# Modulation streams beside an output projection: earlier start, two row tiles a step, half of them on TensorE

## The chip, the cores and the metric

The kernel runs on one core of a Trainium2 chip. The metric is the device time of one execution in microseconds (us); the time of a kernel is the median of its runs. TensorE multiplies matrices, VectorE (DVE), ScalarE (ACT) and GpSimd (POOL) work element by element, SyncE (SP) issues most of the DMA transfers. Each engine takes its own instructions strictly in the order in which they stand in the program, and waits in front of one whose operands are not there yet.

## What is computed

Two layers of a diffusion backbone over 512 latent tokens and 256 context tokens, width 1024, all in 32-bit floats. Layer 0 is a mixer (retention and mLSTM heads) and then a gated feed-forward part. Only the seam between the two matters here:

```
mod = silu(c) @ ada_w[layer] + ada_b[layer]            # 1024 -> 6*1024, the same for c_ctx
sh1, sc1, g1, sh2, sc2, g2 = split(mod, 6)
x   = x + g1 * (concat(retention, mlstm) @ ab_w_out)   # the mixers' output projection
h   = rmsnorm(x, norm_w) * (1 + sc2) + sh2
x   = x + g2 * ((silu(h @ w_gate) * (h @ w_up)) @ ffn_w_out)
```

The same three lines are computed for the context tokens with c_ctx. sc2 and sh2 (columns 32 to 39 and 24 to 31 of the 48 column tiles of mod) are first needed behind the output projection, in the norm ahead of the feed-forward part.

## The kernel before

**Products.** A 32-bit product is made of three TensorE products of rounded parts: each operand is split into a high part (a cast on ACT) and a low part (the rest, a subtraction on DVE). So each 128-column weight unit is loaded by DMA into one of three buffers `wr` (512 KB), cast to `wh` on ACT and subtracted to `wl` on DVE, with three buffers of each.

**The output projection** is `op_out` (from line 1487). It goes through the latent tokens (`LAT`, 512 columns) and then the context tokens (`CTX`, 256 columns); in each, through eight output tiles k. A step is one tile: 8 row tiles by 3 products make 24 matmuls into one PSUM bank `pf`, and `evac` on DVE adds the gated bank to the residual stream `xt`; ACT then squares the new rows and POOL sums the squares into `nacc` for the norm. There are two banks, so step k + 2 waits for the evacuation of step k.

**The modulation streams** (`ada_stream`, from line 700). One stream makes eight column tiles of mod: its weight rows come as eight row tiles `aw` of 128 x 1024 (512 KB each, three buffers, issued on SP). For a row tile k in `on_pe`, TensorE does it directly (`ada_round`: four matmuls of 32 x 256, one for each quarter of the columns). For any other, DVE multiplies the tile by a scalar per partition and adds it to one of two sums `acc` (one for c, one for c_ctx): two instructions of 128 x 1024. In the end two more rounds on TensorE (`ones`) sum each `acc` over the partitions into the same bank `ada`; ACT copies the bank, DVE transposes it and adds the bias (`mod`) and for sc2 the norm weight (`amod`). Streams run one after another. Before, `op_out` starts the stream for sc2 (32) behind step 2 and that for sh2 (24) behind step 5 of LAT, each with row tiles 0 and 1 on TensorE and six on DVE.

**The norm ahead of the feed-forward part** (`norm_seven0`): POOL takes the root of the sums (`rs`), TensorE spreads it over the partitions (`nbc`), DVE writes rows times scale into four tiles `bb` and ACT adds the shift sh2 in place; then come the forms: `two` casts a form's high part on ACT and subtracts its low part on DVE into tiles `g`. The form b11 is the first quarter (upper rows, first 256 columns), b21, b12 and b22 are the others.

**The feed-forward part** begins with `plain()`: two units of gate and up columns, 192 matmuls of 256 columns into `pu`, first with b11 and b21, then with b12 and b22; behind them the context product `pc`. Their weights come through `wr` again, split into `xh`, `xl` (gate) and `wh`, `wl` (up).

**Order of the work.** The program is written by generators that a planner (`Flow`) interleaves by its own estimates of cost, and the tile framework's scheduler may move instructions again when the program is built. So the order on each engine is fixed at build time but stands in no line of the source.

Of the kernel before, what the change touches and what calls it, by code (L numbers as in the profile page):

```python
# [15 lines left out]
P = 128  # L16
# [127 lines left out]
def kernel(ctx, tc, x, c, cx, c_ctx, ada_w, ada_b, norm_w, ffn_w_in, ffn_w_out, ab_w_in,  # L144
# [15 lines left out]
    def nm(s):  # L160
        seq[0] += 1
        return f"{s}_{seq[0]}"
# [3 lines left out]
    def big(shape, dt, name):  # L166
        slots.n -= 1
        return bigp.tile(shape, dt, tag="big", name=nm(name))
# [3 lines left out]
    def psum(name="ps", tag="mx"):  # L172
        return psp.tile([P, 512], F32, tag=tag, name=nm(name))
# [7 lines left out]
    def bank(name):  # L181

        return psum(name, "pj")
# [12 lines left out]
    def order(inst, prev):  # L196
        if prev is not None:
            tc.add_manual_dep(inst.ins, prev.ins.name,
                              mybir.DependencyInfo(mybir.DependencyClass.NoSync, mybir.DependencyReason.DATA),
                              reason="groups of one bank in turn")  # L200
# [10 lines left out]
    def steps(o, pairs, prev=None, cut=12):  # L211

        n = len(pairs)
        m = None
        for i, (l, r) in enumerate(pairs):
            m = pe.matmul(o, l, r, start=(i == 0), stop=(i == n - 1))
            if i == 0:
                order(m, prev)
            if i % cut == cut - 1 and i < n - 1:
                yield  # L220
        return m
# [155 lines left out]
    for i, (lo, hi) in ((1, (2, 4)), (2, (4, 6)), (0, (0, 2))):  # L377
# [4 lines left out]
        for kk in range(4):  # L382
# [3 lines left out]
            for j in range(2):  # L386
                for b in range(2):
                    k = 2 * kk + j
# [221 lines left out]
    def op(gen, specs=()):  # L610

        W.plan(specs)
        prog.append(gen)

    def wfeat(src):
        return src, KT, P

    def pairs_feat(w, c0, ah, al, a, b, ks=KT):
        res = []
        h_, l_ = w  # L620
        for k in range(ks):
            wh, wl = h_[:, k, c0:c0 + P], l_[:, k, c0:c0 + P]
            h, lo = ah(k, a, b), al(k, a, b)
            res += [(wh, h), (wh, lo), (wl, h)]
        return res
# [20 lines left out]
    def evacuated():  # L646

        evac_t.append(flow.cur.t)
        flow.cur.t = evac_t[-2] if len(evac_t) > 1 else 0.0
# [25 lines left out]
    def op_feat(src, acts, evac, parts=(LAT, CTX), before=None, after=None):  # L675

        def gen():
            if before is not None:
                yield from before()
            u, = yield from W.take(1)  # L680
            for part in parts:
                a, b, mc = part
                ps = bank("pf")
                yield from steps(ps[:, 0:b - a], pairs_feat(u, 0, *acts(), a, b))
                if part is parts[-1]:
                    W.give(1)
                evac(part, ps[:, 0:b - a])
                evacuated()
                yield
            if after is not None:  # L690
                after()
        op(gen, [wfeat(src)])
# [3 lines left out]
    def ada_unit():  # L696

        if len(ada_ring["units"]) == 0:
            ada_ask()
        return ada_ring["units"].pop(0)  # L700

    passed, pace = [0], [0]

    def ada_stream(turn, l, t0, on_pe=range(KT), gap=0.0, cols=2, freed=0, every=0):

        yield lambda: ada_turn[1] == turn
        ps = None
        acc = [None] * 2  # L710
        for k in range(KT):
            if every:
                yield lambda: passed[0] >= pace[0]
                pace[0] = max(pace[0], passed[0]) + every
            u, at = ada_unit()
            flow.cur.t = max(flow.cur.t, at)
            yield
            if k in on_pe:
                first = ps is None
                if first:  # L720
                    ps = psum("ada")
                ada_round(ps, k, u, start=first, stop=len(on_pe) == KT and k == KT - 1)
            else:
                for i in range(cols):
                    new = acc[i] is None
                    if new:
                        acc[i] = ada_ring["acc"]()
                    s_ = cmod[:, k, i:i + 1]
                    if new:
                        z = dve.tensor_scalar(acc[i], u, s_, None, ALU.mult)  # L730
                    else:
                        z = dve.scalar_tensor_tensor(acc[i], u, s_, acc[i], ALU.mult, ALU.add)
                    order(z, flow.main)
            slots.n += freed
            ada_ask()
            flow.cur.t = flow.T["pe"] + gap
            yield
        first = ps is None
        if first:
            ps = psum("ada")  # L740
        for i in range(cols if len(on_pe) < KT else 0):
            ada_round(ps, 0, acc[i], ones[:, i, :], first and i == 0, i == cols - 1)
        ada_end(l, t0, KT, ps)
        ada_turn[1] += 1

    def op_ada(l, t0, **how):
        def gen():
            flow.add(ada_stream(ada_turn[0], l, t0, **how), 4, "ada")
            ada_turn[0] += 1
            yield  # L750
        op(gen)
        ada_ring["plan"] += [ada_w[l, P * k:P * k + P, P * t0:P * t0 + D] for k in range(KT)]
# [729 lines left out]
    def op_wait(cond):  # L1482
        def run():
            yield cond
        op_do(run)

    def op_out(wsrc, acts, l, gk, parts, then, adas=()):

        adas = list(adas)
        op_wait(lambda: {(l, 8 * gk), (l, 8 * gk + 4)} <= ada_done)  # L1490
        for part in parts:
            for k in range(KT):
                def evac(part, ps, k=k):
                    a, b, mc = part
                    dve.scalar_tensor_tensor(xk(xt, k, a, b), ps, mod[l][:, 8 * gk + k, mc:mc + 1],
                                             xk(xt, k, a, b), ALU.mult, ALU.add)
                    square_sum(k, a, b)
                op_feat(wsrc[:, P * k:P * k + P], acts, evac, (part,))
                if adas and k % 3 == 2:
                    op_ada(l, adas.pop(0), on_pe=(0, 1))  # L1500
            then(part)

    ready = {}
# [40 lines left out]
    def norm_seven0():  # L1544

        a, b, mc = LAT
        ps2 = psum("nsum")
        for i in range(a // P, b // P):
            pe.matmul(ps2[:, i:i + 1], nacc[:, P * i:P * i + P], cst[:, C_INV:C_INV + 1], start=True, stop=True)
        bcs = yield from rms_bc((ps2[:, a // P:b // P], a // P))  # L1550
        yield lambda: {(0, 24 + t) for t in (0, 4, 8, 12)} <= ada_done
        bb = []

        def two(name, q, src):
            h, lo = form0(0, name, q), form0(1, name, q)
            act.copy(h, src)
            dve.tensor_tensor(lo, src, f(h), ALU.subtract)

        for q in range(4):
            bb.append(big([P, 3, NL], F32, "bb"))  # L1560
            for k in range(2):
                kk = 2 * q + k
                dve.scalar_tensor_tensor(bb[q][:, k], xk(xt, kk, a, b), amod[0][:, 1, kk, 0:1], bcs, ALU.mult, ALU.mult)
                act.activation(bb[q][:, k], bb[q][:, k], AF.Identity, bias=mod[0][:, 24 + kk, 0:1])
        four = [(bb[q][:, 0:2, 0:256], bb[2 + q][:, 0:2, 0:256], bb[q][:, 0:2, 256:512], bb[2 + q][:, 0:2, 256:512],
                 bb[q][:, 2].rearrange("p (k n) -> p k n", k=2)) for q in range(2)]
        for q, (b11, b21, b12, b22, t2) in enumerate(four):
            two("b11", q, b11)
        done0.add("b11")
        yield lambda: "mixed" in done0  # L1570
        for name, i in (("b21", 1), ("b12", 2), ("b22", 3)):
            for q in range(2):
                two(name, q, four[q][i])
            done0.add(name)
            yield
        yield lambda: 0 in done0
        for q, (b11, b21, b12, b22, t2) in enumerate(four):
            dve.tensor_tensor(b11, b11, b12, ALU.subtract)
            dve.tensor_tensor(t2, b22, b11, ALU.add)
        for name in ("t2", "t3", "n1", "n4"):  # L1580
            for q, (b11, b21, b12, b22, t2) in enumerate(four):
                if name == "t3":
                    dve.tensor_tensor(b12, b12, b22, ALU.subtract)
                if name == "n4":
                    dve.tensor_tensor(b21, b21, t2, ALU.subtract)
                two(name, q, {"t2": t2, "t3": b12, "n1": b11, "n4": b21}[name])
            done0.add(name)
            yield
# [827 lines left out]
```

## Time and profile before

| | us |
|---|---|
| median of 3 runs | 1760.28 (1760.05 to 1765.24) |
| profiled execution, its own time | 1761.57 |
| its span, first to last instruction | 1759.8 |
| TensorE busy | 1688.9 (96%) |
| DVE busy | 1213.0 (69%) |
| ACT busy | 754.0 (43%) |
| output projection of layer 0, first to last matmul | 469.8 to 554.1 |
| of it the latent steps | 469.8 to 518.5 |
| first context product of the feed-forward part | 587.6 |

The stage in question is the 118 us from 469.8 to 587.6. A busy share tells little here, since TensorE is busy over most of the span: what counts is where it is idle or at its lower clock, and which instruction ends each such stretch. Matmul rows overlap, so the price of a matmul is the distance between two starts, not its duration.

### The profile page before, as it was taken

Reading aid. Unit: us, or ns where it says so; the run is one execution under the profiler, and the core shown is the slowest. Engines: PE = TensorE matmul, PEld = TensorE weight load, DVE = VectorE, ACT = ScalarE, POOL = GpSimd, SP = SyncE. Lnnn points to the kernel's source line nnn. Section 1 sums busy time; section 2 is a strip of 40 time slices with the busy share of each in tenths; the row PEclk is TensorE's granted clock in tenths of the full one; section 3 lists DMA queues with packets and bytes.
Section 4 is the critical chain, followed back from the end, with each engine's and each line's share of the span. In section 5 each row is a group of like instructions: output and inputs, shape, how many; then the busy total and the mean of one; then the engine's idle time right before and its main releaser. Section 6 shows DMA issues by size and latency. Waiting matters only on the chain.

```text
span 1759.8 us, 31421 instructions
## 1 busy us (share of the span) xinstructions
PE 1688.9 (96%) x12770; PEld 1551.6 (88%) x12770; DVE 1213.0 (69%) x2112; ACT 754.0 (43%) x1406; POOL 305.7 (17%) x308
## 2 busy tenths in 40 slices
PE   7899999999998999999999999799999899999998
PEld 5799899999877998999999998799778899999998
DVE  4845365756588795876657475769765788778785
ACT  4532344433424533333444333545665554344343
POOL 4212120201023001000010102426564300000000
PEclk9999999999999999999999999999999999999999
DMA  9511111011477247466564835322002523333335
GB/s 339 207 52 49 37 37 49 25 37 54 162 217 226 61 144 164 124 167 157 147 164 147 205 122 184 113 73 70 4 1 93 160 73 105 103 105 97 108 86 155
DMA packets 230324, 203.34 MB, mean 116 GB/s; under 512 B 8172, under 2 KB 207268, under 8 KB 230180
## 3 DMA queue, kind: packets, MB, share of 16 engines
q1 hardware_dynamic: 222468, 178.20, 33.1%
q0 software_dynamic: 5760, 18.88, 5.5%
q10 hardware_dynamic: 1952, 4.27, 0.7%
q8 instruction: 100, 1.64, 0.4%
q14 instruction: 44, 0.36, 0.1%
HBM read 178.25 MB, written 23.07 MB: 114 GB/s over the span
## 4 chain that ended last, share of the span: by engine, by line
PE 63%; issue 14%; DVE 10%; DMA 6%; ACT 4%; POOL 2%; SPq 0%; POOLq 0%; ACTq 0%; DVEq 0%
PE pf L107 20%; PE pu L107 12%; PE pt L107 10%; PE pg L107 4%; PE pc L107 4%; DMA wr<-in_ffn_w_in_dram 3%; PE sc L107 3%; DVE acc L107 2%; PE mo L107 2%; PE ao L107 2%; DVE wl L107 2%; DMA xs<-stage 1%; PE atr L107 1%; PE ro L107 1%; PE kv L107 1%
## 5 line engine op out<-in xcount | busy, mean ns | idle before, releaser
L107 PE MATMUL pf<-fu,wh 128*128 128x512 f32 (+1 forms) x1152 | 293.2, 345 | 8.4 <-DVE xt L107 2.8
L107 PEld LDWEIGHTS pf<-fu,wh 128*128 128x128 f32 x1152 | 198.1, 190 | 38.8 <-ACT wh L107 4.7
L107 DVE TENSOR_TENSOR wl<-wr,wh 128x1024 fp32r<-128x1024 f32 (+1 forms) x144 | 173.1, 1203 | 71.4 <-ACT wh L107 69.6
L107 ACT CAST wh<-wr 128x1024 fp32r<-128x1024 f32 (+1 forms) x144 | 143.8, 1001 | 178.7 <-PE pf L107 68.1
L107 PE MATMUL pf<-fu,wl 128*128 128x512 f32 (+1 forms) x576 | 196.0, 342 | 0.0
L107 DVE TENSOR_TENSOR wl<-ws,wh 128x1024 fp32r<-128x1024 f32 x80 | 97.4, 1221 | 57.1 <-ACT wh L107 56.5
L107 PE MATMUL pu<-g,wh 128*128 128x256 f32 x704 | 130.4, 283 | 1.9 <-DVE hfull L107 1.9
L107 ACT CAST xh<-wr 128x1024 fp32r<-128x1024 f32 x84 | 78.4, 946 | 120.6 <-DMA wr<-in_ffn_w_in_dram 71.1
L107 PE MATMUL pc<-g,xh 128*128 128x256 f32 x672 | 123.0, 282 | 1.2 <-ACT stage L107 0.8
L107 ACT CAST wh<-ws 128x1024 fp32r<-128x1024 f32 x80 | 83.5, 1050 | 94.8 <-PE pu L107 47.8
L107 PEld LDWEIGHTS pf<-fu,wl 128*128 128x128 f32 x576 | 109.0, 189 | 13.5
L107 DVE SCALAR_TENSOR_TENSOR acc<-aw,cmod,acc 128x1024 f32<-128x1024 f32 x90 | 117.9, 1335 | 0.1
L107 PE MATMUL pu<-hT,wh 128*128 128x256 f32 x640 | 115.3, 280 | 0.0
L107 PEld LDWEIGHTS pu<-g,wh 128*128 128x128 f32 x704 | 108.9, 190 | 3.4 <-DVE hfull L107 2.1
L107 DVE TENSOR_TENSOR xl<-wr,xh 128x1024 fp32r<-128x1024 f32 x84 | 91.7, 1096 | 21.5 <-ACT xh L107 21.3
L107 PEld LDWEIGHTS pc<-g,xh 128*128 128x128 f32 x672 | 104.1, 190 | 2.0 <-ACT stage L107 1.6
L107 PE MATMUL pu<-g,wl 128*128 128x256 f32 x352 | 99.9, 284 | 0.8 <-DVE wl L107 0.7
L107 PEld LDWEIGHTS pu<-hT,wh 128*128 128x128 f32 x640 | 97.7, 188 | 0.7 <-ACT hT L107 0.2
L1774 POOL DMA_DIRECT2D xs<-stage x32 | 27.9, 871 | 400.2 <-ACT stage L107 381.0
L107 PE MATMUL pc<-g,xl 128*128 128x256 f32 x336 | 94.5, 281 | 0.0
L107 PE MATMUL pu<-hT,wl 128*128 128x256 f32 x320 | 87.7, 281 | 1.5 <-DVE wl L107 1.5
L107 PE MATMUL pt<-wh,hh 128*128 128x256 f32 x288 | 83.3, 291 | 4.1 <-ACT hh L107 2.7
(388 smaller groups left out, 4833.5 us busy)
## 6 DMA issues: line engine op xcount, KB each, us to landing
wr<-in_ffn_w_in_dram SPq DMA_DIRECT2D x88, 512.0 KB, 3.9
aw<-in_ada_w_dram SPq DMA_DIRECT2D x84, 512.0 KB, 5.3
wr<-in_ab_w_in_dram SPq DMA_DIRECT2D x32, 512.0 KB, 4.5
wr<-in_ffn_w_out_dram SPq DMA_DIRECT2D x32, 512.0 KB, 4.1
xs<-stage POOLq DMA_DIRECT2D x32, 384.0 KB, 6.1
wr<-in_ffn_w_out_dram SPq DMA_DIRECT2D x32, 384.0 KB, 4.2
wr<-in_ab_w_out_dram SPq DMA_DIRECT2D x16, 512.0 KB, 4.2
wr<-in_attn_w_out_dram SPq DMA_DIRECT2D x16, 512.0 KB, 4.2
```

Of the source, the lines that this page charges most:

```text
L107: r = fn(*a, **k)
L1774: nc.gpsimd.dma_start(xs2[k // 2, :, NT * (k % 2):NT * (k % 2) + NT], stage[0][:, k % 2], accum_op=ALU.add)
```

## The change

Three things change. `op_out` counts a step in `passed` after each tile and starts the two streams ahead of steps 0 and 1 instead of behind steps 2 and 5. Each stream takes row tiles 0 to 3 on TensorE (before 0 and 1), four on DVE (before six), and with `every=0.5` its row tile k may go on only when int(k / 2) steps have passed since the stream began: two row tiles a step. In `norm_seven0` the rows of `bb` are written in the order in which the forms need them: rows 0 and the b11 forms of them, rows 1 and theirs, then rows 2 and 3; before, all four first.

```diff
@@ ada_stream
         for k in range(KT):
-            if every:
+            if 0 < every < 1:
+                p0 = passed[0] if k == 0 else p0
+                yield lambda: passed[0] >= p0 + int(every * k)
+            elif every:
                 yield lambda: passed[0] >= pace[0]
                 pace[0] = max(pace[0], passed[0]) + every
@@ op_out
+        def step():
+            passed[0] += 1
+
...
-                op_feat(wsrc[:, P * k:P * k + P], acts, evac, (part,))
-                if adas and k % 3 == 2:
-                    op_ada(l, adas.pop(0), on_pe=(0, 1))
+                if adas and k < 2:
+                    op_ada(l, adas.pop(0), on_pe=range(4), every=0.5)
+                op_feat(wsrc[:, P * k:P * k + P], acts, evac, (part,), after=step)
@@ norm_seven0
         for q in range(4):
             bb.append(big([P, 3, NL], F32, "bb"))
+
+        def rows(q):
             for k in range(2):
                 kk = 2 * q + k
...
         for q, (b11, b21, b12, b22, t2) in enumerate(four):
+            rows(q)
             two("b11", q, b11)
         done0.add("b11")
+        for q in (2, 3):
+            rows(q)
         yield lambda: "mixed" in done0
```

Up to the first matmul of the output projection the order of every engine is the same as before. **DVE, from the first evacuation of the output projection on** (`xt<-pf` is an evacuation, `wl` the low part of a weight unit, `acc` a row tile of a stream). Before:

```order
L107 SCALAR_TENSOR_TENSOR xt_4889<-pf_5157,mod_173,xt_4889 128x512
L107 TENSOR_TENSOR wl_5221<-wr_5025,wh_5219 128x1024
L107 SCALAR_TENSOR_TENSOR xt_4889<-pf_5190,mod_173,xt_4889 128x512
L107 TENSOR_TENSOR wl_5256<-wr_5087,wh_5254 128x1024
L107 TENSOR_SCALAR acc_5273<-aw_5152,cmod 128x1024
L107 TENSOR_SCALAR acc_5275<-aw_5152,cmod 128x1024
L107 SCALAR_TENSOR_TENSOR xt_4890<-pf_5225,mod_173,xt_4890 128x512
```

Now:

```order
L107 SCALAR_TENSOR_TENSOR xt_4889<-pf_5157,mod_173,xt_4889 128x512
L107 TENSOR_TENSOR wl_5218<-wr_5025,wh_5216 128x1024
L107 TENSOR_SCALAR acc_5256<-aw_5201,cmod 128x1024
L107 TENSOR_SCALAR acc_5258<-aw_5201,cmod 128x1024
L107 SCALAR_TENSOR_TENSOR acc_5256<-aw_5226,cmod,acc_5256 128x1024
L107 SCALAR_TENSOR_TENSOR acc_5258<-aw_5226,cmod,acc_5258 128x1024
L107 SCALAR_TENSOR_TENSOR xt_4889<-pf_5203,mod_173,xt_4889 128x512
```

The first stream's sums stand one step earlier, and an evacuation of a latent step now stands behind four of them. The last `acc` of the second stream stands ahead of the seventh latent evacuation; before, it stood behind the second context evacuation.

**TensorE, between the sixth and the seventh context step** (`pf_5745` and `pf_5759` are the sixth step's bank, `pf_5780` and `pf_5788` the seventh's, `pu` the feed-forward part's first product). Before:

```order
L107 MATMUL pf_5745<-ml_5139,wh_5723 128x256
L107 MATMUL pf_5745<-mh_5138,wl_5725 128x256
L107 MATMUL pf_5780<-mh_4897,wh_5758 128x256
L107 MATMUL pf_5780<-ml_4898,wh_5758 128x256
L107 MATMUL pf_5780<-mh_4897,wl_5760 128x256
```

Now:

```order
L107 MATMUL pf_5759<-ml_5139,wh_5718 128x256
L107 MATMUL pf_5759<-mh_5138,wl_5720 128x256
L107 MATMUL pu_5883<-g_905_5636,xh_5836 128x256
L107 MATMUL pf_5788<-mh_4897,wh_5753 128x256
L107 MATMUL pf_5788<-ml_4898,wh_5753 128x256
```

The first feed-forward matmul has moved ahead of the last two context steps (six more stand between those two); before, all 192 stood behind the last context step.

**DVE, in the context steps, at the norm's rows** (`bb`). Before:

```order
L107 SCALAR_TENSOR_TENSOR bb_5620<-xt_4889,amod_175,nbc_5615 128x512 x2
L107 SCALAR_TENSOR_TENSOR bb_5625<-xt_4890,amod_175,nbc_5615 128x512 x2
L107 SCALAR_TENSOR_TENSOR bb_5630<-xt_4891,amod_175,nbc_5615 128x512 x2
L107 SCALAR_TENSOR_TENSOR bb_5635<-xt_4892,amod_175,nbc_5615 128x512 x2
L107 STREAM_TRANSPOSE row_5576<-row_5575 128x256
L107 SCALAR_TENSOR_TENSOR xt_4891<-pf_5710,mod_173,xt_4891 128x256
```

Now:

```order
L107 SCALAR_TENSOR_TENSOR bb_5628<-xt_4889,amod_175,nbc_5623 128x512 x2
L107 SCALAR_TENSOR_TENSOR xt_4890<-pf_5689,mod_173,xt_4890 128x256
L107 TENSOR_TENSOR wl_5755<-wr_5605,wh_5753 128x1024
L107 SCALAR_TENSOR_TENSOR bb_5629<-xt_4890,amod_175,nbc_5623 128x512 x2
L107 SCALAR_TENSOR_TENSOR xt_4891<-pf_5724,mod_173,xt_4891 128x256
L107 TENSOR_TENSOR xl_5837<-wr_5722,xh_5836 128x1024
L107 TENSOR_TENSOR g_905_5636<-bb_5628,g_905_5636 128x512
```

The eight row instructions no longer stand in one piece, evacuations and splits stand between them, and the transpose that belongs to sh2 has gone from here: it stands ahead of the last latent evacuation. Behind this place, the order of the later stages differs from before in many small swaps of neighbours; no instruction is added or taken away there.

## Rows read from the trace of the kernel before

**Rows 1.** The page, busy time: engine, us (share of span), instructions.
```profile
PE 1688.9 (96%) x12770; PEld 1551.6 (88%) x12770; DVE 1213.0 (69%) x2112; ACT 754.0 (43%) x1406; POOL 305.7 (17%) x308
```

**Rows 2.** Busy time by stretch, all engines; columns as in the first row.
```profile
core 0: us, PE busy (x) PEld busy (x) DVE busy (x) ACT busy (x) POOL busy (x), PEclk, DMA share, GB/s
469.78:518.53 48.75, 48.75 (x242) 36.75 (x240) 36.70 (x34) 13.44 (x17) 7.61 (x5) 1.00 0.70 219
518.53:525.40 6.87, 3.09 (x24) 2.92 (x24) 6.87 (x9) 2.62 (x3) 2.39 (x1) 0.97 0.66 193
525.40:528.40 3.00, 2.91 (x14) 2.94 (x15) 3.00 (x3) 0.63 (x1) 2.19 (x1) 0.50 0.52 143
528.40:554.10 25.70, 22.33 (x188) 20.70 (x187) 22.47 (x29) 11.25 (x18) 9.16 (x10) 1.00 0.83 263
554.10:559.95 5.85, 0.53 (x4) 0.30 (x3) 2.90 (x4) 5.85 (x11) 1.50 (x3) 0.93 0.88 326
559.95:565.90 5.95, 5.95 (x28) 5.95 (x29) 5.95 (x9) 3.28 (x7) 0.84 (x1) 0.50 0.70 206
565.90:587.62 21.72, 20.47 (x173) 20.27 (x173) 18.23 (x36) 9.67 (x18) 5.31 (x1) 1.00 0.00 1
...
600.00:1105.00 505.00, 496.40 (x3664) 465.11 (x3663) 345.51 (x465) 193.03 (x304) 41.15 (x44) 1.00 0.59 157
1105.00:1760.00 655.00, 629.05 (x4828) 577.52 (x4826) 489.88 (x869) 321.40 (x591) 144.27 (x114) 0.99 0.30 89
```

**Rows 3.** The chain that ended last, 489 to 551 us: start, us, what.
```profile
519.89 3.50 DVE acc L107 x2
...
538.77 9.39 DMA wr<-in_ffn_w_in_dram
```

**Rows 4.** Timeline of TensorE: start, duration, instruction, idle time before and its releaser.
```profile
487.04 0.39 PE L107 MATMUL pf<-mh,wl 128*128 128x512 f32 x1
487.37 0.64 PE L107 MATMUL ada<-aw,cmod 128*32 128x256 f32 x8
487.93 0.50 PE L107 MATMUL pf<-mh,wh 128*128 128x512 f32 x1
...
525.49 0.55 PE L107 MATMUL pf<-mh,wh 128*128 128x256 f32 x1 [3.49 <-DVE xt L107]
...
546.56 0.36 PE L107 MATMUL pf<-mh,wh 128*128 128x256 f32 x1 [1.98 <-DVE xt L107]
...
549.37 0.28 PE L107 MATMUL pf<-mh,wl 128*128 128x256 f32 x1
551.03 0.35 PE L107 MATMUL pf<-mh,wh 128*128 128x256 f32 x1 [1.39 <-ACT wh L107]
...
558.08 0.50 PE L107 MATMUL pu<-g,xh 128*128 128x256 f32 x2 [3.96 <-ACT g L107]
```

**Rows 5.** Row tiles of the streams on DVE, 465 to 540 us: ns min/median/max, starts.
```profile
L107 DVE SCALAR_TENSOR_TENSOR acc<-aw,cmod,acc x20: 1248/1274/2318, 489.5 to 535.9; 128x1024 f32<-128x1024 f32 x20
```

**Rows 6.** Busy time of DVE alone in the first steps.
```profile
469.60:489.50 19.90, 11.69 (x12) 1.00 0.61 199
```

**Rows 7.** Timeline of POOL, DVE and ACT, 526 to 574 us.
```profile
526.21 2.59 POOL L107 TENSOR_TENSOR nacc<-nacc,sq 128x512 f32<-128x512 f32 x1 [3.90 <-ACT sq L107]
...
527.59 2.29 DVE L107 SCALAR_TENSOR_TENSOR acc<-aw,cmod,acc 128x1024 f32<-128x1024 f32 x1
...
550.81 0.17 DVE L107 TENSOR_TENSOR mod<-row,cols_b 128x16 f32<-128x16 f32 x1
...
551.58 4.99 ACT L107 ACTIVATE bb<-bb,mod 128x512 f32<-128x512 f32 x8
...
568.34 5.31 POOL L107 TENSOR_TENSOR rs<-v,mhalf 128x2 f32<-128x2 f32 x1 [6.72 <-DVE v L107]
```

**Rows 8.** Loads of `aw`, 465 to 540 us: issue time in ns, then time to landing.
```profile
L768 SPq DMA_DIRECT2D aw<-in_ada_w_dram x19: 327/328/425, 467.4 to 537.2; - x19
...
DMA to landing us min/median/max: 3.8/4.5/7.5
```

## The prediction, made before the changed kernel ran

> **What bounds the kernel now.** I first read the busy line [rows 1]: TensorE works 96% of the span, so a change pays only where TensorE is idle or at its lower clock. Then I split the stage into stretches [rows 2]. In the latent steps TensorE has no idle time (48.75 of 48.75 us). Behind them it loses: 3.78 us idle ahead of the second context step, 0.09 and 3.37 in the other context steps, 5.32 ahead of the first feed-forward product, 1.25 behind it. That is 13.8 us idle. In two stretches the granted clock is 0.50 (1.2 GHz instead of 2.4): 2.91 and 5.95 us busy, which at full clock would take half, so 4.4 us more are lost. Each follows one of the two longest waits, 3.49 and 3.96 us [rows 4]; the waits of 1.98 and 1.39 us were followed by no such stretch. Together 18.2 us of the 117.8 us from the first projection matmul (469.78) to the first context product (587.62) can be won.
>
> Who ends those waits? The 3.49 and the 1.98 us end with an evacuation `xt` on DVE, the 1.39 us with a cast on ACT, the 3.96 us with a form cast on ACT [rows 4]. DVE is busy in every us of 518.53 to 528.40 [rows 2], and the chain of waits runs there over the streams' sums `acc` [rows 3]: an evacuation stands behind them in DVE's order. The last wait is the same debt, paid later: the shift sh2 is there only at 550.81, ACT's eight row instructions start at 551.58 and take 4.99 us [rows 7], and the first form's cast stands behind them. Meanwhile, from 469.6 to 489.5, DVE was busy 11.69 of 19.90 us [rows 6]. So DVE is idle before the streams and late behind them.
>
> **What the change removes, adds and moves.**
>
> *DVE work.* Of 24 instructions of the two streams 8 go: 8 x 1.274 = 10.2 us [rows 5]. From 469.78 to 528.40, where nearly all 24 lay, DVE was busy 46.6 of 58.6 us [rows 2]; less 10.2 it has some 36 us of work in latent steps of 52 us, and can start on it at once. So it should no longer hold TensorE up: the waits on `xt` (3.49 and 1.98) and the clock stretch behind the first (1.5) go. The 1.39 us on a weight cast goes too if the loads, whose buffers DVE frees, are no longer late; what is late next is ACT, below.
>
> *TensorE work.* Four more rounds. A round's price is the distance of the starts around one, 487.04 to 487.93, less one matmul [rows 4]. With 192 matmuls and six rounds in 48.75 us this gives 0.233 us for a latent matmul and 0.66 for a round; the latent steps get six rounds longer (four of row tiles, two closing ones that stood in the context steps). So they end at 469.8 + 192 x 0.233 + 12 x 0.66 = 522.4 instead of 518.5. The net addition is 4 x 0.66 = 2.6 us. Bounds: 0 if neighbouring rounds overlap, 5.3 if each also waits as long again for its load.
>
> *Loads.* Every row tile still comes once, on the same queue; SP now issues 27 transfers of 512 KB (19 of `aw`, 8 of weights) from 467 to 522, 14 MB or about 260 GB/s, against 219 before [rows 2]. The context steps moved 263 at a DMA share of 0.83, so it fits, but loads will land later than the median of 4.5 us [rows 8]. A load is issued when its buffer's last reader is done, and TensorE's rounds wait in order. With 4.5 us per load I walked down the new DVE order: the fourth row tile is issued at about 475 and read at 481; the first stream's sums end at 492.5 and 494.5, and TensorE wants them at 495.4 and 497; the second stream's end by 519 and are wanted at 520.5. Margins are 1 to 3 us.
>
> *Context steps.* Their stretches held 3.09 + 2.91 / 2 + 22.33 = 26.9 us of work at full clock [rows 2]; less the two closing rounds 25.6. (Eight times the 2.84 us from 546.56 to 549.37 plus one matmul [rows 4] give 22.7; the rest are the norm's small products.) So they end at 522.4 + 25.6 = 548 instead of 554.1. With the shift there at about 523, ACT can take the norm's rows as they come, in pairs between the weight casts, instead of eight in a row. Moving rows 2 and 3 behind the first form costs nothing by itself: they are wanted by b21, 43 matmuls (5.1 us) behind the context steps.
>
> *First feed-forward products.* By the same reckoning their stretches held 0.53 + 5.95 / 2 + 20.47 = 24.0 us of work [rows 2]. I expect about 4 us of waits, three of them from the same walk through the new order: 0.8 for the second unit's weights, 0.4 for b21, 1.6 because the context's sum of squares stands on ACT behind the form casts, and the 1.25 of before for the context's root, which takes 5.31 us on POOL [rows 7]. Their bounds are 0 and the 6.6 + 3.0 us of idle time and lower clock of before; the new order is nearer the lower end, since the forms' inputs are there some 25 us earlier. So the first context product starts near 548 + 24 + 4 = 576 instead of 587.6.
>
> *Behind it.* No instruction changes there. The layer's feed-forward part keeps TensorE busy 496.4 of 505 us and the rest 629.05 of 655 [rows 2], so a shift at its start should pass to the end. But the build reordered these parts in many small swaps; they have 34.6 us of idle time that such swaps could raise or lower. I take 0, with 3 us either way.
>
> *A rule against the change.* While POOL added squares (526.21, 2.59 us), one `acc` on DVE took 2.29 us instead of 1.27 [rows 7]. The Trainium skill, "SBUF — State Buffer", "SBUF: two separate sides", says that a DVE instruction with two SBUF inputs and a GpSimd instruction that reads SBUF lock each other out of a shared port pair for a whole instruction. This trace agrees, with 1.0 us on one instruction. By that rule the sums, which now all lie beside the seven latent additions of squares, could lose about 1 us seven times; the margins above would shrink and the sum would be some 1 us longer. The row shows one such case, and DVE has 16 us to spare, so I leave it at 0.
>
> *The sum.* 18.2 lost now, less 4 still lost, less 2.6 for rounds, is 11.6; the walk says the same, 587.6 - 576 = 11.6. I take 11.5. The profiled execution took 1761.57 (span 1759.8, so 1.8 outside) and would take 1750; it lies 1.3 above the median. The median 1760.28 becomes **1749**.
>
> **The rivals.**
>
> *A: the first feed-forward product becomes the wait.* It now stands on TensorE ahead of the last two context steps, and needs a weight load, its cast, and the form's cast. Its load took 9.39 us before [rows 3] instead of 4.5. By my walk it is issued at 534, so ready at 540, one us ahead of need; at 9.39 it is 4 us late and the two context steps stand behind it. The next gate load follows in the same chain of buffers and costs some 2 us more. For it: the residual stream is stored at that time, and the share was 0.83 to 0.88. Against it: the prefetch of the next stream's row tiles, which was in flight then, now lies earlier. Gain 11.5 - 6 = 5.5: 1755.
>
> *B: the work behind gives it back.* The swaps add up to waits on the chain, or weights come no earlier than before. For it: in the feed-forward part TensorE waits now and then for loads. Against it: it idles only 8.6 us of 505. The shift shrinks to 3 us or less: 1758.
>
> *C, slower: late loads hold the latent steps.* With two banks, step k + 2 waits for the evacuation of step k, and that now stands behind sums that wait for row tiles. If a load lands in 9.4 us as above instead of 4.5, DVE's first two row tiles come at 486 and 489.5, the second evacuation ends at 492.7, and step 4 starts 3.6 us late; each pair of steps repeats it, 12 to 14 us in all, with 4 more from A, against 11.5 won: 4.5 to 6.5 longer, 1766. It decides from a landing time of about 7 us on. Against it: the longest of 19 loads took 7.5 [rows 8], at 219 to 263 GB/s.
>
> *D: more than I take.* No new waits at all, 18.2 - 2.6 = 15.6: 1745.
>
> **How the numbers follow.** Forecast 0.52, A 0.20, B 0.12, C 0.09, D 0.07. A measurement of this kernel tells 0.3% from no change, so the bounds are 1755.0 and 1765.6. The forecast and D lie below, and half of A, so faster has 0.52 + 0.07 + 0.10 = 0.69; the other half of A and B give 0.22 for the same; C gives 0.09 for slower. For the range, what I leave out is C and the far end of D (0.09 + 0.05): 1744 to 1760, which also holds the bounds of the rounds (-2.6 to +2.7 us) and of the swaps (3 us).
>
> **What would show it.** Right: the latent steps last some 52.5 us without idle time; the context steps take about 25 and no evacuation ends a wait over 1 us; the shift is ready before the norm's rows; the lower clock is gone between 520 and 570; the first context product starts near 576. Wrong: TensorE waits for `aw` in the rounds (C), or for `xh` between the sixth and seventh context step (A), or the stage is 11 us shorter and the span is not (B).

## The result and the profile after

| | before | after |
|---|---|---|
| median, us | 1762.58 | 1753.46 |
| ratio after / before, 95% interval | | 0.9947 (0.9935 to 0.9958) |
| profiled execution, its span | 1759.8 | 1750.4 |
| output projection, first matmul | 469.8 | 472.9 |
| first context matmul | 518.9 | 525.8 |
| first context product of the feed-forward part | 587.6 | 580.2 |
| stage between first and last of these | 117.8 | 107.2 |

Both medians were taken side by side, that of before anew; one of its eleven executions took 5717 us, and without it the median is 1762.5. By the ratio the change gains 9.3 us (7.4 to 11.5); the prediction was 11.5, from 1760.28 to 1749. The page's busy line of after, columns as in [rows 1]: TensorE is busy for as long as before, in a shorter span, and DVE has 10.5 us less.

```profile
PE 1688.8 (96%) x12802; PEld 1548.3 (88%) x12802; DVE 1202.5 (69%) x2104; ACT 753.6 (43%) x1406; POOL 300.1 (17%) x308
```

Busy time by stretch in after, to be laid beside [rows 2]: latent steps, context steps with the first products, the rest of the first products, then the two long parts behind.

```profile
core 0: us, PE busy (x) PEld busy (x) DVE busy (x) ACT busy (x) POOL busy (x), PEclk, DMA share, GB/s
472.92:525.50 52.58, 52.58 (x289) 37.36 (x288) 37.45 (x37) 14.03 (x19) 10.17 (x6) 1.00 0.80 253
525.50:553.80 28.30, 27.97 (x236) 27.69 (x234) 23.15 (x32) 16.23 (x25) 9.31 (x11) 1.00 0.78 240
553.80:580.15 26.35, 23.02 (x174) 23.02 (x175) 19.35 (x35) 12.56 (x22) 4.04 (x4) 0.87 0.27 86
580.15:1105.00 524.85, 515.17 (x3836) 483.00 (x3834) 364.44 (x501) 206.51 (x329) 42.42 (x46) 1.00 0.58 154
```

The latent steps still have no idle time on TensorE and are longer by their rounds. The waits on `xt` of [rows 4] are gone, and with them the lower clock between 525 and 528. One wait is left, in the third stretch; TensorE's timeline there (two rows out of it):

```profile
553.19 0.28 PE L107 MATMUL pu<-g,wl 128*128 128x256 f32 x1
557.13 0.58 PE L107 MATMUL pu<-g,xh 128*128 128x256 f32 x1 [3.66 <-ACT g L107]
```

The chain of waits in after leads back from it (start, us, what):

```profile
545.98 0.03 DVE xt L107
546.01 7.59 DMA wr<-in_ffn_w_in_dram
...
553.68 1.04 ACT wh L107
554.73 0.68 ACT bb L107 x2
...
556.57 0.52 ACT g L107
557.09 0.04 issue
557.13 6.94 PE pu L107 x36
```

TensorE waits for a form's cast `g`. It is that of b21, the first behind the two of b11, which started at 542.89 and 545.91. On ACT it stands behind rows of `bb`, and these behind the cast `wh` of the second unit's up weights, whose load was issued at 546.01 and took 7.59 us. ACT works in order, so one late weight load holds up rows and forms that do not need it. Behind the wait the granted clock was 0.50 (1.2 of 2.4 GHz) from 556 to 560 and 0.67 on average from 560 to 564.

What DVE and the loads do now, in three answers (the streams' sums by form; the shift; the loads of `aw` with their median time to landing), to be laid beside [rows 5, 7, 8]:

```profile
L107 DVE SCALAR_TENSOR_TENSOR acc<-aw,cmod,acc x12: 1268/1276/2314, 488.2 to 521.2; 128x1024 f32<-128x1024 f32 x12
```

```profile
526.74 0.16 DVE L107 TENSOR_TENSOR mod<-row,cols_b 128x16 f32<-128x16 f32 x1
```

```profile
aw<-in_ada_w_dram SPq DMA_DIRECT2D x19, 512.0 KB, 4.6
```

The sums end with the latent steps, the shift sh2 is there at 526.7 instead of 550.8, and the loads land as fast as before (5.4 us at the longest).

### The profile page after: what moved, and what is told of

It is laid out like the page before. It is cut to its first block, busy times and chain, and to the rows that moved or that the text cites. A ratio compares the mean times of both kernels' runs of the same rounds, so it can differ in the third digit from the quotient of the medians.

```text
span 1750.4 us, 31471 instructions
## 1 busy us (share of the span) xinstructions
PE 1688.8 (96%) x12802; PEld 1548.3 (88%) x12802; DVE 1202.5 (69%) x2104; ACT 753.6 (43%) x1406; POOL 300.1 (17%) x308
## 4 chain that ended last, share of the span: by engine, by line
PE 70%; issue 13%; DVE 7%; DMA 5%; ACT 4%; POOL 1%; SPq 0%; POOLq 0%; ACTq 0%; DVEq 0%
PE pf L107 24%; PE pu L107 13%; PE pt L107 10%; PE pg L107 5%; PE pc L107 4%; PE sc L107 3%; DMA wr<-in_ffn_w_in_dram 2%; PE ao L107 2%; PE mo L107 2%; DMA xs<-stage 1%; PE ro L107 1%; PE atr L107 1%; PE kv L107 1%; DVE aE L107 1%; DVE wl L107 1%
## 5 line engine op out<-in xcount | busy, mean ns | idle before, releaser
L107 DVE SCALAR_TENSOR_TENSOR acc<-aw,cmod,acc 128x1024 f32<-128x1024 f32 x82 | 105.7, 1316 | 2.7 <-DMA aw<-in_ada_w_dram 2.6
```

Of the source, the lines that this page charges most:

```text
L107: r = fn(*a, **k)
```

## The experiments

Each ratio is to the kernel before, on the same chip (three chips in all); the stage is the time from the first matmul of the output projection to the first context product, from the profiled execution (before 117.8, after 107.2). 1 us is 0.06%.

| kernel | ratio (95%) | stage |
|---|---|---|
| order of the rows alone | 0.9990 (0.9977 to 1.0002) | 116.0 |
| start alone, old order of rows | 0.9963 (0.9949 to 0.9977) | 108.2 |
| share alone, old order | 0.9959 (0.9946 to 0.9973) | 109.6 |
| streams whole, old order | 0.9919 (0.9902 to 0.9937) | 104.4 |
| start and new order | 0.9970 (0.9958 to 0.9982) | 113.7 |
| share and new order | 0.9973 (0.9959 to 0.9986) | 111.6 |
| all of it (after, once more) | 0.9959 (0.9947 to 0.9971) | 107.5 |
| after, stores later | 0.9952 (0.9938 to 0.9966) | 110.0 |
| after, one cast later | 0.9950 (0.9938 to 0.9962) | 105.4 |
| streams whole, context steps first | 0.9926 (0.9915 to 0.9938) | 104.2 |
| stores later, last squares on TensorE | 0.9906 (0.9891 to 0.9921) | 103.1 |
| streams whole, all row tiles on TensorE | 0.9940 (0.9925 to 0.9955) | 110.4 |

### Which part pays: streams or order of rows

The order of the rows alone, on the kernel before:

```diff
+        def rows(q):
             for k in range(2):
...
+            rows(q)
             two("b11", q, b11)
+        for q in (2, 3):
+            rows(q)
```

> The kernel before with one part of the change: the norm's rows in order of need; the streams stay behind steps 2 and 5 with six row tiles on DVE. Theory (the sums on DVE, late in the stage, are the bound): the shift sh2 is still there only near 551 us, so the rows wait for it in any order, and the waits of 3.49 and 1.98 us on xt stay; at best the 3.96 us wait ahead of the first feed-forward product shrinks by the four rows that no longer stand ahead of it (some 2.5 us of ACT): 0 to 3 us faster than before. Rival (the order of the forms makes the gain): 7 us or more faster than before, with the first feed-forward product near 555 without a wait.

As the theory had it, at most 3 us: the gain can't be told from none. The shift came at 542.4, earlier than the 551 I had expected, the second wait on `xt` went, and the wait ahead of the first product shrank to 1.04 us. But the first wait on `xt` stayed, and a new one came behind the forms (two rows of TensorE's timeline):

```profile
525.53 0.45 PE L107 MATMUL pf<-mh,wh 128*128 128x256 f32 x1 [3.48 <-DVE xt L107]
...
563.24 1.01 PE L107 MATMUL nsum<-cst,nacc 128*128 128x1 f32 x4 [2.93 <-POOL nacc L107]
```

The streams whole, with the old order of the rows (the change without its part in `norm_seven0`):

> The changed kernel with the old order of the norm's rows (all four first); streams early, four row tiles on DVE. Theory: the shift is there near 527 us, the waits on xt are gone, so most of the gain stays: 7 to 9 us faster than before; the first feed-forward product stands behind eight rows on ACT and may wait 1 to 2 us more than in the changed kernel. Rival (the order of the forms makes the gain): 3 us faster or less.

It gains 14.2 us, more than the whole change: the interval (0.9902 to 0.9937) ends below both ratios of after (0.9947 and 0.9959), though the first of these has an interval that starts at 0.9935. So neither the theory (7 to 9) nor the rival was right: beside the whole streams the new order of the rows costs some 5 us, or 7 by the second ratio. Only about 3 of them lie in the stage (104.4 against 107.2 and 107.5). In the profiles another 2.0 to 3.3 us lie behind it (1167.0 us from the first context product to the end, against 1170.3 and 1168.9); what makes them no run shows. Here is TensorE's longest wait, and busy time from the first context matmul to the first context product:

```profile
545.97 0.39 PE L107 MATMUL pu<-g,xh 128*128 128x256 f32 x1 [2.80 <-ACT g L107]
```

```profile
527.05:578.65 51.60, 48.53 (x409) 48.11 (x408) 44.98 (x70) 29.48 (x47) 14.09 (x15) 1.00 0.61 176
```

On ACT the eight rows and the forms b11 and b21 now stand ahead of the second unit's two casts. The 3.66 us wait is not there, and the 2.80 us one is followed by the full clock.

### Which part of the streams pays: start or share

```diff
-                    op_ada(l, adas.pop(0), on_pe=range(4), every=0.5)
+                    op_ada(l, adas.pop(0), on_pe=(0, 1), every=0.5)
```

That change to after keeps the early start and undoes the share; the other way round, streams behind steps 2 and 5 with `on_pe=range(4)` undo the start and keep the share.

> The changed kernel, but each stream has only row tiles 0 and 1 on TensorE and six on DVE, as before the change; the streams start early and are paced. Theory (DVE was idle early and late behind the streams: moving is what counts): DVE has some 46 us of work in latent steps of about 50 us, TensorE four rounds less (2.6 us); 5 to 9 us faster than before, perhaps a few waits on xt in the last latent steps. Rival (taking the 10 us of sums off DVE is what counts): within 2 us of before, with waits of over 2 us on xt in the last latent or the first context steps.

> The changed kernel, but its streams start behind steps 2 and 5 as before the change, not paced; four row tiles of each on TensorE, four on DVE. Theory (the start is what counts): DVE is 10 us less late, so the waits on xt shrink from 5.5 us to 1 or 2, but the shift is there only at about 540 us and the form's cast still ends a wait of 1 to 3 us: 3 to 6 us faster than before. Rival (taking the sums off DVE is what counts): as fast as the changed kernel or faster, 9 us or more faster than before.

5.3 and 4.8 us, inside the theories' ranges: each pays about half of after's gain, and neither rival stands. The waits were longer than expected. The start with the new order lost 5.51 us to one of POOL's sums (`nacc`, at 567.47). The share with the new order lost 5.12 us, where 1 to 3 were expected, to a form's cast at 561.57, behind the same `wh`, whose load took 8.88 us there. The same pair with the old order of the rows:

> The kernel before with the streams started ahead of steps 0 and 1 and paced, but two row tiles of each on TensorE and six on DVE, and the old order of the rows: the start alone. With the new order of the rows this start gave 0.997 and the streams whole gave 0.995; the streams whole with the old order gave 0.992. Theory (start and share pay about half each, and the new order of the rows costs some 5 us in either): 0.994 to 0.996 of before, 7 to 10 us faster. Rival (the order of the rows harms only where the streams are whole): 0.997 again, 5 us faster.

> The kernel before with four row tiles of each stream on TensorE and four on DVE, streams behind steps 2 and 5, old order of the rows: the share alone. Theory (DVE is 10 us less late, but the shift still comes behind the latent steps): 0.996 to 0.998 of before, 4 to 7 us faster, with a wait of 2 to 5 us for a form's cast ahead of the first feed-forward product. Rival (the share is what counts): 0.992, as the streams whole.

6.5 and 7.2 us, together 13.7; the streams whole have 14.2. So start and share add up, within the intervals, and each is near its theory's range; for the start the interval holds the rival's 0.997 too. By the ratios the new order costs either of them only 1.2 and 2.5 us, not 5, and neither of these can be told from nothing. The stage does not bear out that it harms most where the streams are whole: there the new order costs 5.5 us beside the start (113.7 against 108.2) and 2.0 beside the share (111.6 against 109.6). The start alone leaves DVE a little late: its sums end a wait of 1.38 us at 525.6. The share alone leaves the shift at 532.8 and a wait of 3.25 us for the form's cast.

All row tiles on TensorE (`on_pe=range(KT)` on the streams whole):

> The streams whole with the old order of the rows, but all eight row tiles of each stream on TensorE and no sums on DVE: 16 rounds instead of 12. Theory (with four tiles on DVE nothing waits for DVE in the latent steps any more, so more rounds only add): the latent steps last 52.84 + 4 x 0.66 = 55.5 us, 2 to 3 us slower than the streams whole, 0.993 to 0.994 of before. Rival (the sums on DVE still cost something in the context steps, by way of late evacuations and loads): as fast as the streams whole or faster.

3.7 us slower than the streams whole in the median ratio (the intervals overlap a little). The latent steps last 55.89 us for 16 rounds instead of 52.84 for 12, so a round costs 0.76 us; another 2.9 us were lost behind, where the theory had none:

```profile
471.37:527.26 55.89, 55.89 (x322) 37.87 (x321) 19.53 (x23) 14.22 (x20) 9.24 (x6) 1.00 0.78 247
```

DVE is busy for only 19.53 of 55.89 us, and nothing is won by it. Half on each engine is the best of the three splits tried.

### Why the new order of the rows costs

After once more, to have it beside the next three:

> The changed kernel once more, on the same chip as the three beside it: 9 us faster than before (0.994 to 0.996). Its profile also tells whether the 3 us that it lost ahead of the output projection (first matmul of it at 472.9 instead of 469.8) come with the kernel or with the run: with the kernel 472 to 474 again, with the run anything from 469 to 474.

It has the same wait, 3.68 us at 557.75, behind a load of 7.65 us, and starts the output projection at 473.5.

The second unit's up cast moved behind the casts of b21 on ACT:

```diff
@@ seven, split
-                act.copy(h, src)
+                z = act.copy(h, src)
+                if job[2] == "eight0" and name == "u":
+                    units0.append(z)
+                    if len(units0) == 2:
+                        order(z, b21_cast[0])
```

> The changed kernel with one instruction moved: on ACT the cast of the second unit's up weights stands behind the casts of b21 instead of ahead of six instructions on which they rest. Theory Q (the new order of the rows is harmful only because this cast waits 3.90 us for its load and holds up everything behind it on ACT): the wait of 3.66 us and the lower clock behind it go, 4 to 6 us faster than the changed kernel, as fast as the kernel that has the streams alone (0.992 of before). Rival (the order of the rows costs elsewhere, or that kernel is faster for another reason): within 1.5 us of the changed kernel, or a new wait for the second unit's weights of over 2 us.

The 3.66 us wait went, as the chain had said. But the kernel is only 1.6 us faster than after in the median ratio, which the intervals do not tell from nothing; the stage is 2 us shorter. Waits of 0.67 us (POOL `nacc`) and 1.15 us (DVE `g`) stand in its place, and the granted clock was still 0.85 from 560 to 570. So the cast explains the wait and 2 of the 3 us by which the stage was longer than with the streams whole (105.4, against 104.4 there), but not the 5 us of the whole time.

The four stores of the residual stream (768 KB each, on POOL's queue) moved behind the context's root:

```diff
+        for kk in range(4):
+            order(nc.gpsimd.dma_start(xs2[kk], ...), root[0])
```

> The changed kernel, with the four stores of the residual stream on POOL's queue moved behind the context's root, to some 15 us later. In the changed kernel a load of the second feed-forward unit, issued at 546.01, took 7.59 us and ended a wait of 3.66 us on TensorE by way of ACT. Theory S (the stores, in flight at that time, make this load late): it lands in some 4.5 us, the wait of 3.66 us and the stretch at the lower clock behind it go: 3 to 6 us faster than the changed kernel, 12 to 15 faster than before. Rival Q (the load is late because it is issued late and shares the queues with the loads around it; ACT's order makes it count): within 1.5 us of the changed kernel.

The load is faster: issued at 545.13, it took 4.78 us, and the wait for the form is 0.74 us. In so far theory S held. Yet the kernel is no faster and the stage 2.7 us longer, for a wait that I had not expected. TensorE's timeline, the chain, and DVE's timeline of this kernel:

```profile
563.49 1.01 PE L107 MATMUL nsum<-cst,nacc 128*128 128x1 f32 x4 [5.59 <-POOL nacc L107]
```

```profile
545.13 4.78 DMA wr<-in_ffn_w_in_dram
...
554.99 7.66 POOL nacc L107
562.64 0.07 issue
562.71 0.73 POOL nacc L107
```

```profile
554.75 0.68 DVE L107 TENSOR_TENSOR bb<-bb,bb 128x512 f32<-128x512 f32 x1
555.35 0.68 DVE L107 TENSOR_TENSOR g<-bb,g 128x512 fp32r<-128x512 f32 x1
555.96 0.68 DVE L107 TENSOR_TENSOR bb<-bb,bb 128x512 f32<-128x512 f32 x1
556.56 2.48 DVE L107 TENSOR_TENSOR g<-bb,g 128x512 fp32r<-128x512 f32 x4
558.97 0.68 DVE L107 TENSOR_TENSOR ws<-wr,wr 128x512 f32<-128x512 f32 x1
559.57 0.68 DVE L107 TENSOR_TENSOR g<-bb,g 128x512 fp32r<-128x512 f32 x1
560.17 0.68 DVE L107 TENSOR_TENSOR ws<-wr 128x512 f32<-128x512 f32 x1
560.77 1.28 DVE L107 TENSOR_TENSOR bb<-bb,bb 128x512 f32<-128x512 f32 x2
564.54 0.16 DVE L107 TENSOR_SCALAR v<-nsum 128x2 f32<-128x2 f32 x1 [2.49 <-PE nsum L107]
```

One addition of squares on POOL takes 7.66 us, and the next, of the same size, 0.73. The long one began 0.24 us after DVE had started on twelve two-input instructions without a gap, and ended 0.6 us after the last of them. The start with the new order shows it too (POOL's timeline; DVE was busy there without a gap from 557.65 to 565.56):

```profile
558.41 7.73 POOL L107 TENSOR_TENSOR nacc<-nacc,sq 128x256 f32<-128x256 f32 x1 [7.47 <-ACT sq L107]
```

So the last experiment on this line takes POOL out of that place: the squares of the last two context steps go as further terms into the small matmuls that add up `nacc` anyway.

```diff
-            pe.matmul(ps2[:, i:i + 1], nacc[...], cst[...], start=True, stop=True)
+            pe.matmul(ps2[:, i:i + 1], nacc[...], cst[...], start=True, stop=not more)
+            for s in more:
+                pe.matmul(ps2[:, i:i + 1], s[...], cst[...], start=False, stop=s is more[-1])
```

> The kernel with the late stores, and with the squares of the last two context steps added up by TensorE, in four small matmuls of the norm's sum, instead of by POOL. With the late stores one such addition took 7.66 us on POOL (554.99 to 562.65) instead of 0.75, while DVE worked without a gap from 554.75 to 562.05, and TensorE waited 5.59 us for it. Theory (POOL stands still while DVE's instructions follow each other without a gap; no other work needs those sums): the wait on nsum goes, and with it the stretch at the lower clock; 5 to 8 us faster than with the late stores alone, 0.991 to 0.992 of before, unless the root, which is POOL's too, now stands still in the same way (then a wait of some 3 us in front of nbc). Rival (the addition was long because its operand came late): the wait on nsum stays at 4 us or more.

It went as the theory said: 0.9906, 8 us faster than the late stores alone, and the best kernel here, 16.5 us faster than before. The root did stand under DVE (2.90 us on POOL), but TensorE did not wait for it. The largest wait left on TensorE, and its busy time from the first context matmul to the first context product:

```profile
557.67 0.38 PE L107 MATMUL nsum<-cst,sq 128*128 128x1 f32 x2 [0.54 <-ACT sq L107]
```

```profile
525.52:575.81 50.29, 49.42 (x418) 49.01 (x416) 43.02 (x69) 29.58 (x47) 14.05 (x12) 1.00 0.55 178
```

0.9 us idle and the full clock throughout, with the new order of the rows. So that order is not bad in itself. It puts rows behind a cast whose load meets the stores (the wait of after), and puts the forms' work on DVE into one piece where the last sums on POOL are wanted (the wait with the late stores; in after TensorE did not wait for POOL). With both out of the way the stage is as short as with the old order (103.1 against 104.4). Whether the old order would gain from the same two changes, and whether the sums on TensorE would do as much without the late stores, was not tried.

The wait of 2.80 us in the streams whole, with the first products held behind the last context matmul:

> The kernel with the streams alone (old order of the rows), and the first feed-forward products held behind the last context matmul on TensorE. There the first product stood ahead of the last two context steps and waited 2.80 us for the form's cast. Theory: those two steps were ready, so the wait goes: 2 to 3 us faster than the streams alone, 16 to 17 faster than before. Rival (the wait is only moved, since DVE and ACT fall behind by as much): as fast as the streams alone, within 1 us.

The rival held: 0.9926 against 0.9919. A wait of 1.68 us came in the context steps and one of 0.69 us ahead of the products. The wait was only moved.

## Why the prediction was right, and where it was off

**DVE was the bound, and could be relieved: right.** Both waits on `xt` and the clock behind the first are gone; DVE has 37.45 us of work in the latent steps (36 forecast). The experiments split the cause as the prediction did not: starting earlier and taking row tiles off DVE each pay about half.

**Latent steps: right.** 52.84 us against 52.6. The six rounds more cost (52.84 - 48.75) / 6 = 0.68 us each, as read (0.66); only the four further ones of all row tiles on TensorE cost 0.76. The loads came at 253 GB/s (260) and landed in 4.6 us, 5.4 at the longest, so rival C had nothing to act on.

**Context steps: right.** From 525.76 to the last of their matmuls, which starts at 550.95, it is 25.2 us (25.6 forecast), with seven products of the next part among them; no evacuation ends a wait. (The side reckoning of 22.7 is read low: from 546.56 to 549.37 plus one matmul it is 2.93 us, so eight times that is 23.4. Nothing hangs on it.)

**First feed-forward products: the term that was too small.** I took 4 us of waits in four places. Two of them (the squares, the root) did not come: the root takes 1.70 us and nothing waits for it. The other two, b21 at 0.4 us and the second unit's weights at 0.8, came as one: TensorE waited 3.66 us for b21, which stood on ACT behind the cast of those weights. The lower clock that followed was not in the sum, so the sign "the lower clock is gone between 520 and 570" failed. Lost in the third stretch: 26.35 - 23.02 = 3.3 us idle and 0.13 x 23.02 = 3.0 us of clock, 6.3 against 4. The step that failed is "moving rows 2 and 3 behind the first form costs nothing by itself": I asked when the rows were wanted, not what they would stand behind on ACT. The time was misread too: between the last context matmul and b21 the trace of after has 19 matmuls (2.2 us); the 43 (5.1 us) hold the 24 of the last context step as well. Rival A had the mechanism, a late load in that stretch that holds up work in order, but looked for it on TensorE at the first product, which did not wait. And the chain of waits names only the load; that one of POOL's sums under DVE can cost as much came out only in other kernels, as when the load was faster.

**Stage, and what lies around it.** The stage is 117.8 - 107.2 = 10.6 us shorter, against 11.5. Behind it 1.9 us more are gained, inside the 3 either way that I allowed. Ahead of it 3.1 us were lost, which I had at 0 because the order there is the same. 10.6 + 1.9 - 3.1 = 9.4, the difference of the spans. The prediction took both outer terms at 0, so it is luck that they nearly cancel.

**The rule that was weighed** cost TensorE nothing, as taken: of twelve `acc` the median is 1.276 us, and two, each begun just behind an addition on POOL, took 2.31. In before it was four of the twenty in [rows 5], of which [rows 7] shows one. In some of the other kernels the price was paid at the other end, by POOL, as told below.

## What to carry to other kernels

When work is moved to where it is needed, ask of each instruction what it will stand behind on its own in-order engine, above all a cast that waits for a load. Undo each part of a change by itself, and in pairs: here the order of the rows was worth nothing alone and minus 5 us beside the streams. A small sum on POOL can take ten times as long while DVE works without a gap; where another engine is adding up anyway, give it the last terms.

## What the runs showed that was not expected

**POOL under DVE.** The addition of 128 x 256 took 0.73 us once DVE had paused, and 7.66 and 7.73 us under DVE's two-input instructions. The Trainium skill, "SBUF — State Buffer", "SBUF: two separate sides", says that such a DVE instruction and a GpSimd instruction that reads SBUF lock each other out of a shared port pair for a whole instruction. The traces agree that one stands while the other works, and show more: in those two kernels POOL got no turn between twelve DVE instructions in a row. It is not always so. In after an addition began in the middle of such a row, took 0.88 us, and it was DVE that paid, with 1.21 us for an instruction that takes 0.68 (POOL's and DVE's timeline):

```profile
560.47 0.88 POOL L107 TENSOR_TENSOR nacc<-nacc,sq 128x256 f32<-128x256 f32 x1 [0.95 <-ACT sq L107]
560.68 1.21 DVE L107 TENSOR_TENSOR g<-bb,g 128x512 fp32r<-128x512 f32 x1
```

What decides between the two no run shows. That the port is the reason is argued, not shown: what the runs show is the overlap, and that the wait goes with the additions. The root's 5.31 us in [rows 7] lie under DVE in the same way; in after it took 1.70.

**The clock.** How long one wait is does not tell what follows. The 2.80 us of the streams whole and the 3.25 us of the share alone were followed by the full clock, and a shorter wait of the share alone, 1.28 us at 565.6, by 0.54 from 567 to 570. The start alone had 2.70 us at the same place, with two of 1.38 and 0.56 us some 19 us ahead of it, and the clock behind it was 0.69 on average:

```profile
545.07:555.00 9.93, 9.93 (x61) 9.93 (x62) 9.43 (x13) 8.98 (x15) 3.61 (x5) 0.69 0.99 272
```

**The start of the program.** The output projection began at 469.8 and 469.4 us in the two kernels whose streams are as before, and between 471.1 and 474.2 in the twelve profiles of the others, although in after every engine's order is the same up to there. The difference goes with stretches at the lower clock between 20 and 200 us, where the granted clock was 0.96 and 0.97 in those two, 0.93 in after and 0.91 in the streams whole. Twelve to two speaks for the kernels, the same order for the single executions; it stays open.
